# First taps of two depthwise convolutions on ScalarE, and the last step of a SiLU on ScalarE and GpSimd

## The chip, the cores and the metric

The kernel runs on one core of one Trainium2 chip. The metric is the device time of one execution in microseconds (us). The program works on TensorE (PE in the profile, with its weight loads as PEld), VectorE (DVE), ScalarE (ACT) and GpSimd (POOL); SyncE (SP) issues all DMAs. Each engine takes its own instructions in the order in which they were laid down, and semaphores hold an instruction back until its inputs are written and its output buffer is free.

## The reference

Two layers of a hybrid block run over 1024 latent tokens and 256 context tokens of width 1024, all in float32. Each layer normalises and modulates its input, multiplies it by a wide `w_in`, and feeds three branches: a state-space scan (SSD) behind a short convolution, attention with grouped keys, and a conformer branch behind a long convolution. The branches are joined by `w_out`. What matters here is cut to this:

```python
def dwconv(x, w, b):                       # one filter per channel
    y = lax.conv_general_dilated(x, w[:, None, :], (1,), [(pad, pad)], ...)
    return y + b

def ssd_branch(z, xbc, ...):
    xbc = jax.nn.silu(dwconv(xbc, conv_w, conv_b))      # 1280 channels, 5 taps
    ...
def conformer_branch(ua, ub, gate, ...):
    u = ua * jax.nn.sigmoid(ub)
    u = jax.nn.silu(layernorm(dwconv(u, conv_w, conv_b), ln_g, ln_b))   # 512 channels, 31 taps
    u = u @ pw_w + pw_b
    return u * jax.nn.silu(gate)
```

The latent and the context tokens are convolved apart, each padded with zeros. The second layer needs only the latent tokens of the conformer branch.

## The kernel before

A layer has three stages: the input projections (`phase_b`), then attention with the SSD scan woven into it, then the output projection. This change lies in the second half of the first of them. There, channels lie on the 128 partitions and tokens along the free dimension. Every product is a float32 matmul made from three passes over operands split in a high and a low part (`mm3`, lines 210 to 216); the weights of one unit are loaded, rounded to the high part on ScalarE and subtracted to the low part on GpSimd (`wblock`, line 359, tile `wtl`).

The loop over `block(i)` (line 623) takes 17 units of 256 channels each. Units with `xbc` hold two 128-channel slices of the short convolution; there are ten slices, j = 0 to 9. Units with `ub, ua` hold one slice of the conformer branch; there are four. The two kinds alternate, so that two slices of `xbc` are followed by one pair `ub, ua`. After these nine units come eight that only make gates (z, gc, ga).

What happens to a unit is this.

- For `xbc` (line 617), ScalarE copies the matmul results into a padded buffer `xpad` (two buffers, zeroed at the pads by GpSimd). `conv_x` (lines 557 to 588) then makes the first tap with one `tensor_scalar` on VectorE (line 562, product and bias), and four more taps with `scalar_tensor_tensor` (line 565, helper line 208). The SiLU is made from a tanh: ScalarE writes tanh of the result into `th` (line 568), and VectorE makes (th + 1) times the result (line 569); weights and bias carry the factor one half. For j below 8, TensorE then transposes the result (line 582) and ScalarE copies the transposes out for the DMA.
- For `ub` (line 601), ScalarE writes a tanh of the matmul results into a tile that shares the tag `th`, and `th` has one buffer. For `ua` (line 610), VectorE makes (th + 1) times the matmul result into the padded `up`.
- `conv_cm` (lines 549 to 555) then makes 31 taps on VectorE, in place in `cac`: the first with `tensor_scalar` (line 552), thirty with `scalar_tensor_tensor` (line 555, helper line 208). `cac` has 1295 columns in the first layer and 1024 in the second. It is read by TensorE later, in `cm_tail` (line 670).

The matmul results go through four PSUM buffers with tag `m`, so TensorE may run at most four tiles ahead of the engine that empties them.

The order on each engine is not the order of the source. `at(us)` sets a priority, and a planner that simulates the program with its own costs lays down, on each engine, whichever ready instruction has the lowest number. Taps of `conv_cm` are 1.7 apart in these numbers, taps of `conv_x` 2 apart, the tanh of `conv_x` comes at 10 and its transposes at 34 behind the unit's matmuls.

Of the kernel before, what the change touches and what calls it, by code (L numbers as in the profile page):

```python
# [10 lines left out]
AF = mybir.ActivationFunctionType  # L11
ALU = mybir.AluOpType
# [148 lines left out]
def build(tc, a, out, depth=DEPTH, dump=None):  # L161
    nc = tc.nc
    es = ExitStack()
    V, S, G, P, Y = nc.vector, nc.scalar, nc.gpsimd, nc.tensor, nc.sync

    def at(us):
        tc.cur_priority = int(us * 100)
# [6 lines left out]
    def mk(p, shape, tag, dt=F32, bufs=None):  # L174
        uid[0] += 1
        k = {} if bufs is None else {"bufs": bufs}
        return p.tile(shape, dt, tag=tag, name=f"{tag}_{uid[0]}", **k)
# [17 lines left out]
    def tr(o, i, idt):  # L195
        P.transpose(o, i, idt)  # L196

    def act(o, i, f, **k):
        S.activation(o, i, f, **k)  # L199

    def ts(e, o, i, s1, op0, s2=None, op1=None):
        if op1 is None:
            e.tensor_scalar(o, i, s1, None, op0)
        else:
            e.tensor_scalar(o, i, s1, s2, op0, op1)  # L205

    def stt(o, i, s, i1, op0, op1):
        V.scalar_tensor_tensor(o, i, s, i1, op0, op1)  # L208
# [101 lines left out]
    def cc(l, n, j=0, w=1):  # L310
        o = CO[n][0] + j * w
        return colc[l][:, o:o + w]
# [36 lines left out]
    def wblock(p, rp, src, tag, bufs, e=None, rtag="wr", rbufs=1):  # L349
        shape = list(src.shape)  # L350
        hi = mk(p, shape, tag + "h", F32R, bufs=bufs)
        lo = mk(p, shape, tag + "l", F32R, bufs=bufs)
        n = shape[1] // 2
        for k in range(2):
            s = slice(n * k, n * k + n)
            raw = mk(rp, [128, n, shape[2]], rtag, bufs=rbufs)
            Y.dma_start(out=raw, in_=src[:, s])
            act(hi[:, s], raw, AF.Copy)
            (e or G).tensor_tensor(lo[:, s], raw, hi[:, s].bitcast(F32), ALU.subtract)  # L359
        return hi, lo  # L360
# [73 lines left out]
    def phase_b(l, nh, b0, pp):  # L434
# [74 lines left out]
        w = wblock(wt, wt, a["wtm"][l, 1], "wt", 2, V)  # L509
# [3 lines left out]
        for i, j in enumerate((2, 0, 1)):  # L513
            u0 = b0 + 52 + 26 * i
            at(u0 - 20)
            w = wblock(wt, wt, a["wtd"][l] if j == 2 else a["wtm"][l, 2 + j], "wt", 2, V)
# [23 lines left out]
        cw = mk(up_p, [128, 4, 31], "cmw")  # L540
        sw = mk(xp_p, [128, 60], "scw")
# [5 lines left out]
        NCM = 1024 if last else 1295  # L547

        def conv_cm(j, t0, pace):
            u, o = ups[j], cac[j]  # L550
            at(t0)
            ts(V, o[:, 0:NCM], u[:, 0:NCM], cw[:, j, 0:1], ALU.mult, cc(l, "cmb", j), ALU.add)
            for k in range(1, 31):
                at(t0 + k * pace)
                stt(o[:, 0:NCM], u[:, k:k + NCM], cw[:, j, k:k + 1], o[:, 0:NCM], ALU.mult, ALU.add)

        def conv_x(j, t0):
            xp = xps[j]
            at(t0)
            o = mk(xp_p, [128, 1282], "xcv", bufs=2)  # L560
            w = sw[:, 5 * j:5 * j + 5]
            ts(V, o, xp[:, 0:1282], w[:, 0:1], ALU.mult, sw[:, 50 + j:51 + j], ALU.add)
            for k in range(1, 5):
                at(t0 + 2 * k)
                stt(o, xp[:, k:k + 1282], w[:, k:k + 1], o, ALU.mult, ALU.add)
            at(t0 + 10)
            th = mk(up_p, [128, 1282], "th")
            act(th, o, AF.Tanh)
            stt(o, th, 1.0, o, ALU.add, ALU.mult)
            if j >= 6:  # L570
                d = bT_d[j - 6] if j < 8 else cT_d[j - 8]
                Y.dma_start(out=d[:, 0:1024], in_=o[:, 0:1024])
                Y.dma_start(out=d[:, 1024:1280], in_=o[:, 1026:1282])
            if j < 8:
                at(t0 + XLAG)
                sg = mk(gp, [128, NT, 128], "xsg")
                for ta in (0, 4, 8):
                    n = min(4, NT - ta)
                    ps = mk(*((pt, [128, 4, 128], "t") if ta == 4 else (px, [128, 4, 128], "x")))
                    for t in range(ta, ta + n):  # L580
                        c0 = t * 128 + (2 if t >= 8 else 0)
                        tr(ps[:, t - ta, :], o[:, c0:c0 + 128], idf)
                    act(sg[:, ta:ta + n, :], ps[:, 0:n, :], AF.Copy)
                if j < 6:
                    d = xt_d[:, :, 128 * j:128 * j + 128]
                else:
                    d = bt_d[:, :, 128 * (j - 6):128 * (j - 6) + 128]
                Y.dma_start(out=d.rearrange("t p f -> p t f"), in_=sg)
# [34 lines left out]
        def block(i):  # L623
            u = FM_UNITS[i]
            u0 = b2 + 26 * i
            at(u0 - 20)
            w = wblock(wt, wt, a["wfm"][l, i], "wt", 2)
            tt = u0
            for m, (n, j) in enumerate(u):
                full = n == "xbc" or not last  # L630
                for t0, tn in ((0, 512), (512, 512), (1024, 256)):
                    if t0 >= 1024 and not full:
                        continue
                    at(tt)
                    ps = mk(pm, [128, 512], "m")
                    mm3(ps[:, 0:tn], lambda x, k: w[x][:, k, 128 * m:128 * m + 128],
                        lambda x, k: h[x][:, k, t0:t0 + tn], KT)
                    fm_fin(ps, n, j, t0, tn)
                    tt += 5.2 * tn / 512
                if n == "ua":  # L640
                    conv_cm(j, tt, CM_PACE)
                if n == "xbc":
                    conv_x(j, tt)
# [563 lines left out]
```

## Time and profile before

| | |
|---|---|
| time, median of 3 runs | 2924.92 us (2923.34 to 2926.68) |
| the profiled execution's own time | 2925.86 us |
| its span in the trace | 2924.0 us |
| busy over the span: PE, DVE, ACT, POOL | 95%, 74%, 37%, 40% |
| mean granted TensorE clock | 0.976 |

The span runs from the first to the last instruction that was recorded; 1.86 us of the profiled time lie around it. "Busy" is a share of the whole span and hides that the stages have different limits: VectorE is at 9 tenths or more in the convolutions of both layers (about 300 to 605 us and 1814 to 2078 us), and far below that in the gate units behind them. A busy time contains the time in which an instruction has started and is held up inside, so a long duration of a short instruction is itself a sign of something. PEclk is the share of full speed that TensorE was granted.

In timelines a row has the start, the duration, the engine, the line, the operation, the tiles written and read, the shape and the count; a bracket gives the idle time of the engine before it and what ended it. In tables of groups a row has the count, the busy time and the mean duration in ns, then the idle time before. In tables of waits a row has who waited for whom: the total, the number of times and the longest.

### The profile page before, as it was taken

The numbers are of one execution on the slowest core, as the hardware profiler recorded it, in microseconds if no ns is written. First come the engines' busy times: TensorE is split into PE (matmuls) and PEld (weight loads), VectorE is DVE, ScalarE is ACT, GpSimd is POOL, SyncE is SP. The second block draws the span as 40 slices with busy tenths as digits, with TensorE's granted clock in tenths as the row PEclk, the third lists the DMA queues.
The fourth block names the chain that finished last, engine by engine and source line by source line (L and its number), as shares of the span: only waits on it lengthen the run. The fifth ranks groups of instructions, "written<-read, shape, count | busy, mean of one in ns | idle before, by whom it ended". The sixth has DMA issues, their size and how long they took to land. (4 is left out here: it accounts for less than half of the span.)

```text
span 2924.0 us, 41060 instructions
## 1 busy us (share of the span) xinstructions
PE 2775.7 (95%) x15708; PEld 2058.5 (70%) x15708; DVE 2167.2 (74%) x2987; ACT 1068.0 (37%) x1801; POOL 1167.3 (40%) x832
## 2 busy tenths in 40 slices
PE   5999998999999999899999999999998999999998
PEld 3888876888855555565787998877886565555676
DVE  4576899973288889887545577999834889898744
ACT  4212221222245555454335322222223455644532
POOL 2244122232166767662112353122322676775111
PEclk8999998999999999999999999999999999999999
DMA  6541111223342323223745322113335232321654
GB/s 237 191 160 66 56 55 62 92 92 112 101 144 84 102 68 104 67 76 99 213 153 161 122 77 68 56 55 98 111 118 168 74 98 77 95 64 43 185 154 144
DMA packets 284035, 314.44 MB, mean 108 GB/s; under 512 B 27606, under 2 KB 219190, under 8 KB 282814
## 3 DMA queue, kind: packets, MB, share of 16 engines
q1 hardware_dynamic: 283838, 311.82, 33.5%
q8 instruction: 123, 2.02, 0.3%
q14 instruction: 74, 0.61, 0.1%
HBM read 236.25 MB, written 75.50 MB: 107 GB/s over the span
## 5 line engine op out<-in xcount | busy, mean ns | idle before, releaser
L193 PE MATMUL m<-hh,wth 128*128 128x512 f32 (+1 forms) x1440 | 534.9, 371 | 0.1
L193 PE MATMUL m<-hl,wth 128*128 128x512 f32 (+1 forms) x1440 | 533.4, 370 | 0.0
L193 PE MATMUL m<-hh,wtl 128*128 128x512 f32 (+1 forms) x1440 | 532.7, 370 | 0.0
L199 ACT ACTIVATE a_p<-m 128x512 f32<-128x512 f32 x492 | 289.0, 595 | 374.0 <-PE m L193 370.6
L208 DVE SCALAR_TENSOR_TENSOR cac<-up,cmw,cac 128x1295 f32<-128x1295 f32 (+1 forms) x240 | 385.4, 1627 | 2.0
L935 DVE TENSOR_REDUCE a_sm<-m 128x1 f32<-128x512 f32 (+1 forms) x600 | 332.5, 582 | 46.9 <-PE m L193 45.0
L359 POOL TENSOR_TENSOR wtl<-wr,wth 128x1024 fp32r<-128x1024 f32 x68 | 200.3, 2945 | 406.6 <-ACT wth L199 406.6
L193 PE MATMUL t<-a_p,vs 128*64 128x256 f32 x1968 | 324.0, 405 | 0.7 <-DVE a_rc L1010 0.3
L193 PEld LDWEIGHTS m<-hh,wth 128*128 128x128 f32 x1440 | 274.0, 190 | 48.0 <-ACT th L199 0.5
L193 PEld LDWEIGHTS m<-hh,wtl 128*128 128x128 f32 x1440 | 273.5, 190 | 48.3
L193 PEld LDWEIGHTS m<-hl,wth 128*128 128x128 f32 x1440 | 273.8, 190 | 47.4
L193 PE MATMUL m<-q_a,k_a 128*128 128x512 f32 (+1 forms) x656 | 259.7, 406 | 6.1 <-DVE a_sm L935 4.6
L193 PE MATMUL m<-k_a,q_a 128*128 128x512 f32 (+1 forms) x600 | 247.0, 437 | 13.6 <-DVE a_sm L935 9.8
L193 PE MATMUL m<-woh,yh 128*128 128x512 f32 x576 | 225.8, 395 | 8.2 <-issue 3.3
L193 PE MATMUL m<-woh,yl 128*128 128x512 f32 x576 | 228.8, 398 | 4.4 <-DVE yl L1099 4.3
L193 PE MATMUL m<-wol,yh 128*128 128x512 f32 x576 | 226.5, 394 | 0.0
L193 PE MATMUL m<-q_b,k_b 65*128 65x512 f32 (+1 forms) x656 | 218.8, 344 | 0.0
L193 PEld LDWEIGHTS m<-q_a,k_a 128*128 128x128 f32 x656 | 125.9, 192 | 107.1 <-issue 52.0
L193 PEld LDWEIGHTS t<-a_p,vs 128*64 128x64 f32 x1968 | 104.3, 136 | 133.9 <-issue 95.3
L193 PEld LDWEIGHTS m<-k_a,q_a 128*128 128x128 f32 x600 | 113.5, 195 | 113.3 <-issue 45.2
L199 ACT ACTIVATE wth<-wr 128x1024 fp32r<-128x1024 f32 (+1 forms) x84 | 89.3, 1064 | 256.3 <-DMA wr<-in_wfm 134.5
L193 PE MATMUL m<-wth,hh 128*128 128x256 f32 (+1 forms) x608 | 173.7, 288 | 0.6 <-DVE c_qn L474 0.5
(239 smaller groups left out, 5604.4 us busy)
## 6 DMA issues: line engine op xcount, KB each, us to landing
wr<-in_wfm SPq DMA_DIRECT2D x68, 512.0 KB, 3.6
s_cb<-cum_d SPq DMA_DIRECT2D x72, 384.0 KB, 3.7
ada_w<-in_adaw SPq DMA_DIRECT2D x32, 512.0 KB, 4.2
wor<-in_wout SPq DMA_DIRECT2D x64, 256.0 KB, 3.1
s_x<-xt_d SPq DMA_DIRECT2D x38, 384.0 KB, 3.0
yf<-ys_d SPq DMA_DIRECT2D x36, 384.0 KB, 4.0
yf<-ya_d SPq DMA_DIRECT2D x36, 384.0 KB, 4.2
yf<-yc_d SPq DMA_DIRECT2D x36, 256.0 KB, 2.9
```

Source lines behind the costliest of these rows:

```text
L193: P.matmul(o, l, r, start=start, stop=stop)
L199: S.activation(o, i, f, **k)
L208: V.scalar_tensor_tensor(o, i, s, i1, op0, op1)
L359: (e or G).tensor_tensor(lo[:, s], raw, hi[:, s].bitcast(F32), ALU.subtract)
L935: V.tensor_reduce(sm[:, 2 * x + t, j:j + 1], ps[:, 0:kn], axis=AX.X, op=ALU.max)
```

## The change

Four instructions change in the source, in `conv_cm` and `conv_x`.

- The first tap of `conv_cm` (four times a layer) is an activation with function Identity on ScalarE, with the tap as its scale and the bias as its bias, where it was a `tensor_scalar` on VectorE.
- The first tap of `conv_x` (ten times a layer) likewise.
- The last step of the SiLU in `conv_x` (ten times a layer) was one `scalar_tensor_tensor` on VectorE. It is now an Identity with bias 1 on ScalarE, in place in `th`, and a `tensor_tensor` product on GpSimd.

No tile, buffer, priority or DMA is changed. The planner makes its orders anew.

```diff
         def conv_cm(j, t0, pace):
             u, o = ups[j], cac[j]
             at(t0)
-            ts(V, o[:, 0:NCM], u[:, 0:NCM], cw[:, j, 0:1], ALU.mult, cc(l, "cmb", j), ALU.add)
+            act(o[:, 0:NCM], u[:, 0:NCM], AF.Identity, scale=cw[:, j, 0:1], bias=cc(l, "cmb", j))
             for k in range(1, 31):
                 at(t0 + k * pace)
                 stt(o[:, 0:NCM], u[:, k:k + NCM], cw[:, j, k:k + 1], o[:, 0:NCM], ALU.mult, ALU.add)
@@
             w = sw[:, 5 * j:5 * j + 5]
-            ts(V, o, xp[:, 0:1282], w[:, 0:1], ALU.mult, sw[:, 50 + j:51 + j], ALU.add)
+            act(o, xp[:, 0:1282], AF.Identity, scale=w[:, 0:1], bias=sw[:, 50 + j:51 + j])
             for k in range(1, 5):
                 at(t0 + 2 * k)
                 stt(o, xp[:, k:k + 1282], w[:, k:k + 1], o, ALU.mult, ALU.add)
             at(t0 + 10)
             th = mk(up_p, [128, 1282], "th")
             act(th, o, AF.Tanh)
-            stt(o, th, 1.0, o, ALU.add, ALU.mult)
+            act(th, th, AF.Identity, bias=1.0)
+            G.tensor_tensor(o, th, o, ALU.mult)
```

## Prediction

> **What bounds the kernel now.** I read the page first, for the whole, then busy time by stretch, because the change touches one stage of each layer only.
>
> ```profile
> span 2924.0 us, 41060 instructions
> PE 2775.7 (95%) x15708; PEld 2058.5 (70%) x15708; DVE 2167.2 (74%) x2987; ACT 1068.0 (37%) x1801; POOL 1167.3 (40%) x832
> ...
> 300.00:400.00 100.00, 95.85 (x493) 81.08 (x492) 98.29 (x61) 21.80 (x34) 24.15 (x19) 0.98 0.18 58
> 400.00:500.00 100.00, 80.99 (x402) 67.92 (x401) 96.50 (x63) 20.00 (x31) 20.63 (x17) 0.88 0.20 65
> 500.00:605.00 105.00, 102.66 (x530) 86.77 (x529) 103.39 (x72) 19.97 (x30) 24.40 (x7) 1.00 0.23 79
> ...
> 600.00:800.00 200.00, 197.41 (x1051) 168.29 (x1050) 79.82 (x158) 45.92 (x74) 44.99 (x31) 0.99 0.31 106
> ...
> 1900.00:2000.00 100.00, 90.33 (x412) 73.87 (x411) 99.89 (x70) 24.04 (x34) 26.05 (x22) 0.95 0.24 75
> ```
>
> The columns are the stretch, its length, busy time of PE, PEld, DVE, ACT and POOL, the granted clock, and the DMA's share and rate. TensorE sets the time nearly everywhere. In the convolutions (300 to 605, and about 1814 to 2078) VectorE is full and TensorE has holes, while behind them (600 to 800) VectorE falls to 40% and TensorE is full again. The waits of TensorE, 300 to 605 and then 1814 to 2079, say who makes the holes; the row between them is VectorE's only wait from 300 to 605:
>
> ```profile
> PE x L196 <- DVE xcv L208: 13.3, 2, 11.1
> PE x L196 <- ACT xsg L199: 5.7, 3, 4.9
> PE t L196 <- DVE xcv L208: 4.2, 1, 4.2
> PE t L196 <- DVE cac L208: 2.3, 1, 2.3
> ...
> DVE up L208 <- PE m L193: 5.9, 4, 2.7
> ...
> PE t L196 <- DVE xcv L208: 11.7, 3, 6.1
> PE t L196 <- DVE cac L208: 1.2, 1, 1.2
> ```
>
> So 25.5 us in the first layer and 12.9 us in the second are waits for the convolutions, 38.4 us in all. That is the most that a lighter VectorE can give, beside a little clock: 0.88 over 100 us says that some of that stretch ran slowly around its holes.
>
> **What VectorE saves.** Groups, 300 to 605 us, with GpSimd's products for scale, then one row of the second layer:
>
> ```profile
> L205 DVE TENSOR_SCALAR xcv<-xpad,scw 128x1282 f32<-128x1282 f32 x8 | 16.0, 1998 | 0.0
> L208 DVE SCALAR_TENSOR_TENSOR xcv<-th,xcv 128x1282 f32<-128x1282 f32 x8 | 11.9, 1485 | 0.0
> L205 DVE TENSOR_SCALAR cac<-up,cmw,colc 128x1295 f32<-128x1295 f32 x4 | 5.9, 1469 | 0.1
> ...
> L359 POOL TENSOR_TENSOR wtl<-wr,wth 128x1024 fp32r<-128x1024 f32 x19 | 67.9, 3573 | 180.9 <-ACT wth L199 180.8
> ...
> L205 DVE TENSOR_SCALAR cac<-up,cmw,colc 128x1024 f32<-128x1024 f32 x4 | 5.4, 1361 | 0.1
> ```
>
> Read plainly, 16.0 + 11.9 + 5.9 = 33.8 us go. But the means of the first taps are not their price, as the rows below show. (Two of the ten slices come before 300 us, where VectorE has room; they count nothing.)
>
> **What GpSimd's product costs VectorE.** No product of GpSimd stands here on these tiles; the nearest is `wtl`, the same operation on 1024 columns. Timeline:
>
> ```profile
> 338.56 2.55 POOL L359 TENSOR_TENSOR wtl<-wr,wth 128x1024 fp32r<-128x1024 f32 x1 [4.74 <-ACT wth L199]
> 338.78 3.69 DVE L208 SCALAR_TENSOR_TENSOR cac<-up,cmw,cac 128x1295 f32<-128x1295 f32 x1
> ...
> 460.10 8.98 POOL L359 TENSOR_TENSOR wtl<-wr,wth 128x1024 fp32r<-128x1024 f32 x1 [17.65 <-ACT wth L199]
> ...
> 548.43 2.66 POOL L359 TENSOR_TENSOR wtl<-wr,wth 128x1024 fp32r<-128x1024 f32 x1 [4.71 <-ACT wth L199]
> 548.75 0.68 DVE L208 SCALAR_TENSOR_TENSOR g_o<-g_t,m 128x512 f32<-128x512 f32 x1
> 549.35 3.10 DVE L208 SCALAR_TENSOR_TENSOR xcv<-xpad,scw,xcv 128x1282 f32<-128x1282 f32 x1
> ```
>
> The tap that meets `wtl` takes 3.69 us, where the same tap alone takes 1.56 (row 352.63 below): it ends 1.36 us after GpSimd, so it began when GpSimd was done. `g_o`, with one input in PSUM, runs beside GpSimd in 0.68 us; the tap behind it waits. GpSimd and a tap take turns, then, and the other way round GpSimd waits too: 8.98 us where 2.55 do. The slow first taps are such meetings, and when they are gone the next tap meets `wtl` in their place. A first tap's own price is 0.94 us (row 368.33 below; 0.80 for 1024 columns).
>
> The ledger of VectorE, first layer: off go 8 x 0.94 + 4 x 0.94 + 8 x 1.49 = 23.2 us. On come eight products. One costs 3.69 - 1.56 = 2.13 us for 1024 columns, so 2.67 for 1282, and 21.3 us for eight. Net -1.9 us. Second layer: 8 x 0.94 + 4 x 0.80 + 8 x 1.49 = 22.6, net -1.3. The bounds of one product are nothing, where VectorE stands idle anyway, and its whole length, 2.55 x 1282/1024 = 3.2: net between -23.2 and +2.4. I take 2.67, because VectorE has 5.9 us of idleness in 305.
>
> The Trainium skill has this as a rule (SBUF — State Buffer, section "Who interferes with whom"): a VectorE instruction with two SBUF inputs contends with a GpSimd instruction that reads SBUF, and whichever starts first holds the shared ports for its whole length. The trace agrees: 3.69 us with two SBUF inputs, 0.68 with one. By the rule each product that starts first costs the whole 3.2, 4.2 us more per layer than I count.
>
> **What the longer chain costs TensorE.** The hand-over of slices 2 and 3 to TensorE in the first layer, and the same in the second:
>
> ```profile
> 349.91 1.27 ACT L199 ACTIVATE th<-xcv 128x1282 f32<-128x1282 f32 x1 [11.43 <-DVE xcv L208]
> 351.22 1.49 DVE L208 SCALAR_TENSOR_TENSOR xcv<-th,xcv 128x1282 f32<-128x1282 f32 x1
> 352.63 1.56 DVE L208 SCALAR_TENSOR_TENSOR cac<-up,cmw,cac 128x1295 f32<-128x1295 f32 x1
> 352.75 1.36 ACT L199 ACTIVATE th<-m 128x512 f32<-128x512 f32 x3 [1.08 <-DVE xcv L208]
> 352.77 1.12 PE L196 MATMUL t<-msk,xcv 128*128 128x128 f32 x4 [4.15 <-DVE xcv L208]
> 354.11 0.68 DVE L208 SCALAR_TENSOR_TENSOR up<-th,m 128x512 f32<-128x512 f32 x1
> 360.80 0.69 DVE L208 SCALAR_TENSOR_TENSOR up<-th,m 128x512 f32<-128x512 f32 x1 [1.32 <-PE m L193]
> 364.48 0.41 DVE L208 SCALAR_TENSOR_TENSOR up<-th,m 128x256 f32<-128x256 f32 x1
> 364.81 3.59 DVE L208 SCALAR_TENSOR_TENSOR cac<-up,cmw,cac 128x1295 f32<-128x1295 f32 x1
> 368.33 0.94 DVE L205 TENSOR_SCALAR cac<-up,cmw,colc 128x1295 f32<-128x1295 f32 x1
> ...
> 1864.48 1.28 ACT L199 ACTIVATE th<-xcv 128x1282 f32<-128x1282 f32 x1 [11.22 <-DVE xcv L208]
> 1868.36 0.66 PE L196 MATMUL t<-msk,xcv 128*128 128x128 f32 x4 [2.11 <-DVE xcv L208]
> 1868.40 1.09 ACT L199 ACTIVATE th<-m 128x512 f32<-128x512 f32 x2 [2.65 <-DVE xcv L208]
> 1869.41 0.68 DVE L208 SCALAR_TENSOR_TENSOR up<-th,m 128x512 f32<-128x512 f32 x1
> ```
>
> One instruction, the finish at 351.22, frees everything: the transposes on TensorE, and the single `th` buffer into which ScalarE empties three PSUM buffers of `ub`. From tanh to TensorE it takes 2.86 us, in the second layer 3.88. Now come tanh 1.27, Identity, which I price like the tanh on the same shape, 1.27, 0.1 for the extra hand-over (as between tanh and finish here), and the product. For it I take the mean of `wtl` with its waits, 3.573 x 1.252 = 4.47 (bounds 3.2, and 8.98 - 2.55 = 6.4 of waiting more). Together 7.1 us: +4.2 in the first layer, +3.2 in the second. The even slices hand over with room to spare and pay nothing here.
>
> TensorE's delay comes back: the second `up` waits for it already (1.32 us). Per hand-over in the first layer VectorE gains 2 x 0.94 + 1.49 - 2.67 = 0.7 on the way to it, loses 4.2, and gains 0.94 at the first tap of `conv_cm`. That tap waits on ScalarE for the last `up`; the tap of the previous slice (364.81, 3.59 us) covers its 1.27. Without that cover, 1.5 us of idleness take the place of the 0.94. So +2.6 each, and three make +7.7. The last pair, which hands nothing to TensorE, adds 2 x 2.67 - 2 x 0.94 - 2 x 1.49 = +0.5: +8.2. In the second layer the first `up` has 0.46 us of room (1869.41 behind the first half of the pair at 1868.40): -0.7 + 3.2 - 0.46 - 0.80 = +1.2 each, three +3.7, last pair +0.5: +4.2. TensorE waits for the last tap of `cac` at both ends (2.3 and 1.2 us above), so both delays pass on whole.
>
> **What costs nothing.** ScalarE gets 24 more instructions a layer of some 1.27 us, 31 us in a stretch of 305 where it is busy for about 62; nothing on its queue is late but by waiting. The first tap of `conv_x` has its buffers early. Behind that of `conv_cm` stand the next emptyings of `xpad`, with four PSUM buffers in between. Behind the product on GpSimd stand `wtl` (TensorE has no wait for weights above) and pads. The stores of B and C wait on SyncE some 4 us longer with weight loads behind them; that same missing wait is their cover, and without it up to 4 us each would show.
>
> **The sum.** 2925.86 (the profiled execution, 0.94 above the median of the runs and inside their spread) + 8.2 + 4.2 = 2938.3 us. I forecast 2938. With bare products (no wait, 5.8 us for the chain) each of six hand-overs is 1.3 better: 2930. With 2.8 us more of waiting each, half-way between the mean and the worst: 2955.
>
> **The rivals.**
>
> *The room is real (faster).* If the products fall where VectorE stands idle, 23.2 and 22.6 us are truly off. Spread over four pairs that is 5.8 a pair: by the third hand-over 17.4 - 4.2 = 13.2 ahead, and 2.3 at the last tap: -15.5. In the second layer 17.0 - 3.2 = 13.8 exceeds the 11.7 of waits, with 1.2 at the end: -12.9. Together 2897. It decides from the point where a product costs VectorE less than 1.49 + 0.94. For it speaks that VectorE is truly the bound; against it the 3.69 us row. Half of it gives 2911.
>
> *The fillers go (much slower).* Between hand-over and next slice VectorE lives on old taps: seven in the first layer (10.9 us), three of 1.28 in the second (3.8). A planner that takes VectorE to be lighter may lay them ahead of the hand-over. All gone costs 3 x 10.9 + 3 x 3.8 = 44 us, half of it 22, on top of the sum: 2960 to 2982. Against it: no priority is changed.
>
> *It is hidden (no change).* If the new order puts other taps where the chain is longer, the nets remain, -3.2 us: 2923.
>
> **How the numbers follow.** Forecast 0.50 (own range 2930 to 2955), the room is real 0.17, the fillers go 0.13, hidden 0.20. Two runs of this kernel can be told apart from about 0.2%, here 5.8 us. Slower: 0.45 of the first, all 0.13, and 0.02 of hidden, 0.60. Faster: 0.17 and 0.03 of hidden, 0.20. Same: the rest, 0.20. The range 2908 to 2962 leaves out most of the faster case (0.11), the upper half of the fillers (0.06) and 0.02 of the forecast.
>
> **What would show it.** In the profile after, products of GpSimd on `xcv` of about 3.2 us or more, and beside each a tap of some 4.2 us (1.56 + 2.67); about 21 us a layer of such excess. TensorE's transposes of `xcv` waiting for GpSimd, over 25.5 and 11.7 us in total; `up` waiting more than 5.9 us. VectorE's busy share from 300 us to the end of the convolutions unchanged. I am wrong if taps beside the products keep 1.56 us, if TensorE's waits shrink, or if ScalarE's first taps hold up the emptying of PSUM.

## The result, and the profile after

The changed kernel takes 2950.56 us, the median of 4 runs (2946.96 to 2955.21), where the kernel before takes 2924.43 (2923.34 to 2926.68, 4 runs). The ratio is 1.0089, with a 95% interval of 1.0072 to 1.0107: slower by 0.9%. The profiled execution took 2949.53 us, 23.67 more than the profiled execution before. Its page and its busy time by stretch, in the columns of the prediction:

```profile
span 2947.8 us, 41130 instructions
PE 2775.8 (94%) x15708; PEld 2059.3 (70%) x15708; DVE 2131.5 (72%) x2939; ACT 1131.6 (38%) x1849; POOL 1232.2 (42%) x852
...
300.00:400.00 100.00, 92.64 (x477) 78.19 (x477) 99.19 (x57) 31.31 (x41) 26.06 (x21) 0.97 0.16 52
400.00:500.00 100.00, 82.25 (x412) 69.14 (x411) 99.47 (x55) 28.79 (x38) 32.05 (x22) 0.90 0.20 65
500.00:605.00 105.00, 98.13 (x497) 83.31 (x497) 98.31 (x71) 25.70 (x33) 38.45 (x11) 0.97 0.22 75
...
1900.00:2000.00 100.00, 86.05 (x412) 71.25 (x411) 99.36 (x62) 29.43 (x35) 31.13 (x24) 0.95 0.15 52
```

VectorE has 48 instructions less and is as full as it was wherever the convolutions run; over the whole span it is lighter by 36 us. TensorE has the same 2776 us of work and more holes.

Where the time lies is read from one group of matmuls, the first pass of the input projections. Its first and last start in a layer mark the stage. Rows of the tile view, the kernel before, each layer in a window of its own (count, shortest, median and longest in ns, first and last start; the shapes of a large group are those of a sample):

```profile
L193 PE MATMUL m<-hh,wth x816: 274/392/775, 241.6 to 799.0; 128*128 128x512 f32 x109, 128*128 128x256 f32 x55
L193 PE MATMUL m<-hh,wth x624: 274/392/775, 1762.2 to 2226.0; 128*128 128x512 f32 x136, 128*128 128x256 f32 x20
```

The same for the changed kernel:

```profile
L193 PE MATMUL m<-hh,wth x816: 274/392/776, 240.1 to 804.7; 128*128 128x512 f32 x109, 128*128 128x256 f32 x55
L193 PE MATMUL m<-hh,wth x624: 274/392/792, 1768.7 to 2248.7; 128*128 128x512 f32 x136, 128*128 128x256 f32 x20
```

The first layer's stage grew from 557.4 to 564.6 us, +7.2; the second layer's from 463.8 to 480.0, +16.2. Together this is 23.4 of the span's 23.8 us. Below, "the two stages" means the sum of these two lengths: 1021.2 us before, 1044.6 after.

The waits of TensorE in the changed kernel, first 300 to 612 us, then 1814 to 2092:

```profile
PE x L196 <- ACT xsg L199: 19.1, 3, 7.5
PE t L196 <- DVE cac L208: 6.9, 1, 6.9
PE x L196 <- POOL xcv L570: 6.0, 3, 2.0
...
PE t L196 <- POOL xcv L570: 17.7, 3, 7.3
PE t L196 <- DVE cac L208: 9.0, 1, 9.0
```

The rows for `xsg` belong to the hand-overs: ScalarE's copies of an even slice's transposes stand in its order behind the tanh and Identity of the odd slice (in the first one below, at 351.77 behind 350.60), and TensorE needs the PSUM buffer that they empty. With them the hand-overs of `xcv` hold TensorE for 25.1 us in the first layer (23.2 before) and 17.7 us in the second (11.7 before). The wait for the last tap of `cac` went from 2.3 to 6.9 us and from 1.2 to 9.0. So there are two sources, and the larger is the second: +7.9 us at the hand-overs, +12.4 us at the end of the long convolution. Together 20.3 of 23.4. The other 3 us are no idleness: in the two stages TensorE is busy 985.7 us for the same matmuls, 982.6 before. That fits the first matmuls behind a wait, which take longer than later ones of the same kind (0.78 us at 356.71 and 0.39 at 358.12, both shown below).

Now the pieces. GpSimd's product on an even slice, and the tap beside it (timeline of the changed kernel), then the groups, 300 to 605 us:

```profile
331.55 3.85 POOL L570 TENSOR_TENSOR xcv<-th,xcv 128x1282 f32<-128x1282 f32 x1 [0.34 <-ACT th L199]
332.61 4.16 DVE L208 SCALAR_TENSOR_TENSOR cac<-up,cmw,cac 128x1295 f32<-128x1295 f32 x1
...
L208 DVE SCALAR_TENSOR_TENSOR cac<-up,cmw,cac 128x1295 f32<-128x1295 f32 x120 | 230.4, 1932 | 3.8 <-ACT cac L199 1.9
L208 DVE SCALAR_TENSOR_TENSOR xcv<-xpad,scw,xcv 128x1282 f32<-128x1282 f32 x32 | 59.7, 1866 | 0.0
L570 POOL TENSOR_TENSOR xcv<-th,xcv 128x1282 f32<-128x1282 f32 x8 | 28.7, 3591 | 12.2 <-ACT th L199 12.2
```

The tap ends 1.37 us after the product, so it ran when GpSimd was done, as the tap beside `wtl` did before. Eight taps of the first layer carry such an excess, 20.7 us over their own price, and eight of the second, 20.5. The same 120 and 32 taps took 209.6 and 53.1 us before: they are 27.4 us dearer now, a part of it meetings with `wtl` that fell on the first taps before. VectorE's busy time from 300 to 605 us is 297.0 us, against 298.2; the second window holds some gate work too, since the convolutions now end earlier.

The hand-over of slices 2 and 3 in the first layer, and one of the second:

```profile
349.12 8.87 DVE L208 SCALAR_TENSOR_TENSOR cac<-up,cmw,cac 128x1295 f32<-128x1295 f32 x4
349.29 1.27 ACT L199 ACTIVATE th<-xcv 128x1282 f32<-128x1282 f32 x1 [13.37 <-DVE xcv L208]
350.60 1.27 ACT L199 ACTIVATE th<-th 128x1282 f32<-128x1282 f32 x1
352.01 3.02 POOL L570 TENSOR_TENSOR xcv<-th,xcv 128x1282 f32<-128x1282 f32 x1 [2.52 <-ACT th L199]
355.06 1.36 ACT L199 ACTIVATE th<-m 128x512 f32<-128x512 f32 x3 [1.55 <-POOL xcv L570]
355.09 1.12 PE L196 MATMUL x<-msk,xcv 128*128 128x128 f32 x4 [1.99 <-POOL xcv L570]
356.71 0.78 PE L193 MATMUL m<-hh,wth 128*128 128x512 f32 x1
357.91 0.68 DVE L208 SCALAR_TENSOR_TENSOR up<-th,m 128x512 f32<-128x512 f32 x1
...
1869.92 1.28 ACT L199 ACTIVATE th<-xcv 128x1282 f32<-128x1282 f32 x1 [11.59 <-DVE xcv L208]
1872.65 3.75 POOL L570 TENSOR_TENSOR xcv<-th,xcv 128x1282 f32<-128x1282 f32 x1 [2.54 <-ACT th L199]
1876.43 0.60 ACT L199 ACTIVATE th<-m 128x512 f32<-128x512 f32 x1 [3.92 <-POOL xcv L570]
```

From tanh to the first emptying behind it: 5.77 us (355.06 - 349.29), 2.84 before; 6.51 in the second layer, 3.92 before. But VectorE does not wait behind it. At 349.12 it has four old taps in front of the `up`, and reaches that `up` at 357.91, 2.85 us after its input was begun.

The `cac` wait has another origin. Between the third hand-over and the transposes that wait for `cac`, TensorE has projections. Their count before, first and second layer (windows 494.0 to 604.8 and 1985.7 to 2078.0):

```profile
L193 PE MATMUL m<-hh,wth x178: 274/392/775, 496.0 to 602.3; 128*128 128x512 f32 x120, 128*128 128x256 f32 x58
L193 PE MATMUL m<-hh,wth x132: 274/392/775, 1986.4 to 2075.9; 128*128 128x512 f32 x116, 128*128 128x256 f32 x16
```

And after (windows 494.5 to 595.2 and 1999.7 to 2081.4), with the spacing of such matmuls:

```profile
L193 PE MATMUL m<-hh,wth x153: 274/392/775, 496.5 to 587.9; 128*128 128x512 f32 x104, 128*128 128x256 f32 x49
L193 PE MATMUL m<-hh,wth x108: 274/392/774, 2000.4 to 2072.1; 128*128 128x512 f32 x92, 128*128 128x256 f32 x16
...
358.12 0.39 PE L193 MATMUL m<-hh,wth 128*128 128x512 f32 x1
358.81 0.40 PE L193 MATMUL m<-hh,wth 128*128 128x512 f32 x1
```

In the new order the transposes stand 16 matmuls of 512 columns and 9 of 256 earlier in the first layer, 24 of 512 earlier in the second. Each stands for three passes, 0.69 us at 512 columns: some 14 us (16 x 0.69 + 9 x 0.35) and 17 us (24 x 0.69) of work that used to lie ahead of them. VectorE's last tap came earlier too, but by less. Before, then after, first layer:

```profile
L208 DVE SCALAR_TENSOR_TENSOR cac<-up,cmw,cac x120: 1550/1559/3707, 300.6 to 603.3; 128x1295 f32<-128x1295 f32 x120
```

```profile
L208 DVE SCALAR_TENSOR_TENSOR cac<-up,cmw,cac x120: 1550/1565/4169, 299.9 to 593.7; 128x1295 f32<-128x1295 f32 x120
```

It is 9.6 us earlier, the transposes 14: the difference is the 4.6 us by which that wait grew. In the second layer the last tap ends 3.5 us later (2078.0 before, 2081.5 after), although the whole stage began 6.5 later, so VectorE is 3.0 us ahead there. The hand-overs hold TensorE back by 6.0 more. 17 - 3.0 - 6.0 leaves about the 7.8 by which that wait grew.

### The profile page after: what moved, and what is told of

It reads as the page before. It is cut to its first block, busy times and chain, and to the rows that moved or that the text cites. A ratio compares the mean times of both kernels' runs of the same rounds, so it can differ in the third digit from the quotient of the medians.

```text
span 2947.8 us, 41130 instructions
## 1 busy us (share of the span) xinstructions
PE 2775.8 (94%) x15708; PEld 2059.3 (70%) x15708; DVE 2131.5 (72%) x2939; ACT 1131.6 (38%) x1849; POOL 1232.2 (42%) x852
## 5 line engine op out<-in xcount | busy, mean ns | idle before, releaser
L208 DVE SCALAR_TENSOR_TENSOR cac<-up,cmw,cac 128x1295 f32<-128x1295 f32 (+1 forms) x240 | 433.0, 1817 | 7.6 <-ACT cac L199 3.7
L359 POOL TENSOR_TENSOR wtl<-wr,wth 128x1024 fp32r<-128x1024 f32 x68 | 193.7, 2849 | 259.1 <-ACT wth L199 248.1
```

## The experiments

Each was timed in several rounds against the kernel before on the same chip. In the first four runs the kernel before took 2928.19 us (median of 22 runs, 2918.36 to 2934.26), in the last four 2927.14 (median of 32, 2917.03 to 2937.46). These runs scatter more than those of the result, and only the ratios are compared. Diffs are against the changed kernel.

### The first taps alone, the SiLU as before

```diff
-            act(th, th, AF.Identity, bias=1.0)
-            G.tensor_tensor(o, th, o, ALU.mult)
+            stt(o, th, 1.0, o, ALU.add, ALU.mult)
```

> The first taps of both convolutions on ScalarE, the SiLU's last step left on VectorE as before. Theory (GpSimd and VectorE's taps take turns; the longer chain from tanh to TensorE; transposes of cac that TensorE's order has earlier): neither the product nor the longer chain is here. VectorE loses 8 x 0.94 + 4 x 0.94 = 11.3 us in the first layer and 10.7 in the second, and nothing comes on. The waits of TensorE shrink by most of that: 2905 to 2912 us, faster than before by 13 to 20. Taps of 4.2 us are gone, those of 3.6 us beside wtl stay. Rival (the 14 first taps on ScalarE hold up the emptying of PSUM or make VectorE wait): some half of the 26 us that the whole change lost, 2935 to 2940.

Measured: 2918.15 us, ratio 0.9970 (0.9954 to 0.9985). The two stages take 1010.1 us, 11.1 less than before, but in this one execution the attention between them took 8.9 us longer (972.1 against 963.2); see the table of steps below. The hand-overs of the first layer hold TensorE for 14.5 us instead of 23.2, but the wait for `cac` rose to 3.8 us there and to 6.7 us in the second layer. In the second layer TensorE also waits 4.3 us for ScalarE to empty a PSUM buffer into `th`. So this half of the change is worth 0.3%, somewhat less than expected.

### The SiLU alone, the first taps as before

```diff
-            act(o[:, 0:NCM], u[:, 0:NCM], AF.Identity, scale=cw[:, j, 0:1], bias=cc(l, "cmb", j))
+            ts(V, o[:, 0:NCM], u[:, 0:NCM], cw[:, j, 0:1], ALU.mult, cc(l, "cmb", j), ALU.add)
...
-            act(o, xp[:, 0:1282], AF.Identity, scale=w[:, 0:1], bias=sw[:, 50 + j:51 + j])
+            ts(V, o, xp[:, 0:1282], w[:, 0:1], ALU.mult, sw[:, 50 + j:51 + j], ALU.add)
```

> The SiLU's last step on ScalarE and GpSimd, the first taps left on VectorE. Theory: each of ten products a layer costs a tap beside it 2.6 us and saves 1.49, so VectorE is heavier than before by 8 x 1.1 = 9 us a layer in the full stretch, and the chain to TensorE is longer by 4 us at each of six hand-overs: slower than the whole change or like it, 2950 to 2965 us. Rival (ScalarE's first taps are what cost): 2930 to 2938, between before and the whole change.

Measured: 2964.72 us, ratio 1.0117 (1.0099 to 1.0134), inside the expectation; the two stages take 1052.9 us, 31.7 more than before. The loss is in the SiLU alone, and the taps give back a part of it.

### The product on VectorE

```diff
-            G.tensor_tensor(o, th, o, ALU.mult)
+            V.tensor_tensor(o, th, o, ALU.mult)
```

> The whole change, but the SiLU's product is made by VectorE; th + 1 stays on ScalarE. Theory: no product of GpSimd, so no turn-taking; VectorE loses only its first taps, 11 us a layer; the chain to TensorE is longer than before by one ScalarE instruction, 1.3 us, at six hand-overs: 2908 to 2920 us, faster than before. Taps of 4.2 us are gone. Rival (ScalarE's 24 instructions a layer cost, wherever the product is): 2945 to 2955, like the whole change.

Measured: 2930.55 us, ratio 1.0004 (0.9994 to 1.0015). The turns with GpSimd's product are gone (those with `wtl` stay), and so is most of the loss, but the gain of the first taps did not come out either: the expectation was missed by 10 us. The third hand-over of the first layer in this run shows one reason:

```profile
482.02 5.26 DVE L208 SCALAR_TENSOR_TENSOR cac<-up,cmw,cac 128x1295 f32<-128x1295 f32 x2
482.19 1.27 ACT L199 ACTIVATE th<-xcv 128x1282 f32<-128x1282 f32 x1 [1.69 <-DVE xcv L208]
483.49 1.27 ACT L199 ACTIVATE th<-th 128x1282 f32<-128x1282 f32 x1
487.20 1.49 DVE L570 TENSOR_TENSOR xcv<-th,xcv 128x1282 f32<-128x1282 f32 x1
488.72 1.36 ACT L199 ACTIVATE th<-m 128x512 f32<-128x512 f32 x3 [2.56 <-DVE xcv L570]
```

The chain is 6.53 us long here. Two taps fill the two activations, they meet `wtl`, and the product stands behind them until 487.20. Where nothing is met the chain is 4.43 us, still 1.6 longer than before: one activation of 1.27 us more, and its hand-overs.

### The tail of the long convolution 20 priority units later

`cm_tail` holds the transposes of `cac`.

```diff
-TAIL = 40.0
+TAIL = 60.0
```

> The whole change, with the conformer's tail laid 20 later in priority (TAIL 60 for 40), which puts the transposes of cac into TensorE's order about where they were before the change. Theory: the two waits of TensorE for the last tap of cac (6.9 and 9.0 us, 2.3 and 1.2 before) go, because TensorE has 2.4 and 2.6 tiles of 5.6 us more to do ahead of them: 12 to 16 us faster than the whole change, 2935 to 2940. What is left of the loss is the hand-overs of xcv. Rival (the delay is VectorE's and only shows there): TensorE waits elsewhere instead, no change, 2948 to 2953.

Measured: 2937.07 us, ratio 1.0030 (1.0017 to 1.0043). The waits of TensorE in this run, first and second layer:

```profile
PE x L196 <- ACT xsg L199: 18.7, 3, 6.7
PE x L196 <- POOL xcv L570: 6.0, 3, 2.0
PE m L193 <- DVE g_o L208: 1.2, 1, 1.2
...
PE t L196 <- POOL xcv L570: 16.7, 3, 6.9
```

The hand-overs are as long as in the changed kernel, and the waits for `cac` are gone. The two stages take 1027.9 us, 16.7 less than those of the changed kernel; the ratio is 0.59% lower. That is the share of the early transposes in the changed kernel.

It is the share in this kernel only, because the planner moved them furthest here. The number of `m<-hh,wth` matmuls from the start of the stage to the transposes that need the last tap is, for the first and second layer:

| run | matmuls ahead |
|---|---|
| kernel before | 546, 452 |
| first taps alone | 544, 440 |
| product on VectorE | 542, 441 |
| SiLU alone | 537, 436 |
| changed kernel | 521, 428 |
| changed kernel, late tail | 544, 448 |

With both parts of the change, which take the most off VectorE, the transposes come earliest.

### The same late tail with the first taps alone, and with the kernel before

> First taps on ScalarE, SiLU as before, and the conformer's tail 20 later in priority. Theory: the taps-only kernel gained 10 us instead of 13 to 20 because TensorE's order had the transposes of cac 1.5 tiles earlier in the second layer and waited 3.8 and 6.7 us for the last taps. Laid one tile later there, the 6.7 goes almost wholly, the 3.8 stays in part: 6 to 8 us faster than taps-only, 2910 to 2914 beside a kernel before of 2928, ratio about 0.994 to 0.996; faster than both kernels. Rival (VectorE's end sets it, wherever the wait shows): as taps-only, ratio 0.997.

> The kernel before with the conformer's tail 20 later in priority and nothing else. Theory: TensorE waits for cac only 2.3 and 1.2 us there, so at most 3.5 us can be had: ratio 0.998 to 1.000. Rival (a late tail is worth some 13 us on any kernel, and has nothing to do with the change): ratio about 0.996.

Measured: 2916.88 us, ratio 0.9970 (0.9958 to 0.9981), and 2927.87 us, ratio 1.0005 (0.9994 to 1.0017). The late tail does nothing for the kernel before, so the 0.59% are no general gain of a later tail. For the first taps alone the expectation was missed: the `cac` wait of the second layer is gone in the profile, and the two stages are 4.0 us shorter than without the late tail (1006.1 against 1010.1), but the ratio is the same. 4 us are 0.14%, and these intervals cannot tell them. The late tail had little to move there, 1 and 8 matmuls against 23 and 20 in the changed kernel. The ratio is that of the rival, which this run does not refute.

### Half a product

GpSimd multiplies columns 0 to 640 only; the late tail stays.

```diff
-            G.tensor_tensor(o, th, o, ALU.mult)
+            G.tensor_tensor(o[:, 0:641], th[:, 0:641], o[:, 0:641], ALU.mult)
```

> The whole change with the late tail, and GpSimd multiplies only the first 641 of the 1282 columns (the other columns stay without the SiLU's factor). TensorE's order has the transposes of cac at the same places as in the whole change with the late tail. Theory: the cost goes with the length of the product. Taps beside it take 2.9 us where 4.2 were (1.55 + half of 2.6); the excess is 10 us a layer where it was 20.6; the chain from tanh to TensorE is 1.5 us shorter, 4.3 and 5.0 us. Together 8 to 15 us faster than the whole change with the late tail (ratio 1.003): ratio 0.998 to 1.000. Rival (an instruction more on GpSimd and ScalarE and their hand-overs cost, whatever the length): ratio 1.003, unchanged.

Measured: 2923.89 us, ratio 0.9990 (0.9981 to 0.9998). One product of it:

```profile
353.40 1.66 POOL L570 TENSOR_TENSOR xcv<-th,xcv 128x641 f32<-128x641 f32 x1 [2.53 <-ACT th L199]
```

The cost goes with the length of the product: 0.40% lie between this run and the full product with the same tail (1.0030). No count of instructions or of hand-overs differs between the two. A tap that meets only such a half product takes 1.2 us more than its own price, where one beside a full product took 2.6 more.

### The product on VectorE, with the late tail

> The whole change with the late tail and the product on VectorE, nothing of it on GpSimd. Again the transposes of cac lie at the same places. Theory: no excess of taps beside products; chain 4.4 and 5.2 us as in the run with the product on VectorE; the waits for cac (4.1 and 7.5 us there) go: ratio 0.995 to 0.998, faster than that run (1.0004) by 8 to 11 us, and slower than taps-only with the late tail by some 4 to 8 us, for one ScalarE instruction at six hand-overs. Rival (ScalarE's extra instructions are what costs): ratio 1.003.

Measured: 2928.19 us, ratio 1.0002 (0.9991 to 1.0013). The late tail gave nothing here, and the expectation was missed. It had only 2 and 7 matmuls to move, and the waits for `cac` fell from 4.1 and 7.5 us to 2.5 and 2.5 without a gain in time. With the transposes late, one more activation in the chain still takes back all that the first taps give.

Three of these runs have the transposes of `cac` at the same place in TensorE's order, within one matmul, and differ in the SiLU only. Their stages, from the tile view. The first taps alone:

```profile
L193 PE MATMUL m<-hh,wth x816: 274/392/776, 243.7 to 790.5; 128*128 128x512 f32 x109, 128*128 128x256 f32 x55
L193 PE MATMUL m<-hh,wth x624: 274/392/796, 1757.5 to 2216.8; 128*128 128x512 f32 x136, 128*128 128x256 f32 x20
```

With Identity and the product on VectorE:

```profile
L193 PE MATMUL m<-hh,wth x816: 274/392/775, 241.7 to 794.0; 128*128 128x512 f32 x109, 128*128 128x256 f32 x55
L193 PE MATMUL m<-hh,wth x624: 274/392/775, 1767.3 to 2231.2; 128*128 128x512 f32 x136, 128*128 128x256 f32 x20
```

With Identity and the product on GpSimd:

```profile
L193 PE MATMUL m<-hh,wth x816: 274/392/775, 241.6 to 799.2; 128*128 128x512 f32 x109, 128*128 128x256 f32 x55
L193 PE MATMUL m<-hh,wth x624: 274/392/776, 1768.4 to 2238.7; 128*128 128x512 f32 x136, 128*128 128x256 f32 x20
```

So the way from the kernel before to the changed one can be walked in four steps. The first column is one profile each, the second the ratios of the runs.

| step | two stages | ratio |
|---|---|---|
| first taps on ScalarE, late tail | 1021.2 to 1006.1: -15.1 | -0.30% |
| Identity ahead of the product (on VectorE) | to 1016.2: +10.1 | +0.32% |
| the product from VectorE to GpSimd | to 1027.9: +11.7 | +0.28% |
| the tail back at 40, transposes early | to 1044.6: +16.7 | +0.59% |
| sum | +23.4 | +0.89% |

The second column times 2927 us is -8.8, +9.4, +8.2 and +17.3. Both agree but for the first step, where the two stages show more than the runs. By the whole spans of these profiles (2924.0, 2916.2, 2926.7, 2935.0 and 2947.8 us) the steps are -7.8, +10.5, +8.3 and +12.8: the first now agrees, because the attention between the two stages took 967.0 us there and 963.2 before. It took 973.3, 969.2 and 964.0 in the next three. Whether that follows from the edits or is scatter of single executions is open, so the last step is worth between 12.8 us (spans) and 17.3 (ratios).

The table is one order of the steps, and the steps depend on each other. With the tail at 40 the product's move from VectorE to GpSimd costs 0.85% (1.0004 to 1.0089), and it also brings the transposes 21 and 13 matmuls further ahead. Of the 10.1 us of the second step, 5.6 are idleness of TensorE and 4.6 the same matmuls taking longer, so the waits of the longer chain show for about half of it.

## Why the prediction was right, and where it was not

The direction and its first cause held: the forecast was 2938 against 2950.56 measured, the gain taken off VectorE was eaten by the product, and the hand-overs became longer. Its size was half of the measured one, for one step that failed. That the time still fell so close in the first layer is luck: the sum led the cost through a delay of VectorE that did not occur.

*GpSimd's product beside a tap: held.* 2.67 us each was forecast, 21.3 us for eight; 20.7 and 20.5 were measured. The ledger held too: from the first tap of `conv_cm` with two inputs to the end of the last, taps and SiLU together take 2.7 us less of VectorE's time in the first layer and 0.9 less in the second, where -1.9 and -1.3 were forecast. The Trainium skill says the same of such a move (Perfetto Trace Analysis, section "Optimizing Scalar/DVE Operations"): offloading between GpSimd and VectorE might not help, because they share a read port. The runs agree: with the late tail, the product is 0.28% cheaper on VectorE than on GpSimd.

*The chain: right in kind, too long.* 7.1 us was forecast, 5.77 and 6.51 were measured. The mis-sized term is the product with its waits, 4.47 us by the mean of `wtl`; inside the hand-overs it took 3.01 to 3.76. `wtl` as a mean contains long waits that no product inside a hand-over met. (The upper bound's 2.8 us of waiting, half-way between the mean of 4.47 and the worst of 3.2 + 6.4 = 9.6, is 2.6 by these numbers, and its 2955 is 2954; nothing hangs on it.)

*TensorE's delay comes back into VectorE: wrong.* `up` was to wait more than 5.9 us. VectorE's waits of 300 to 605 us have no row for `up` any more; the one row for `cac` is this:

```profile
DVE cac L208 <- ACT cac L199: 1.9, 1, 1.9
```

The planner laid more old taps ahead of the hand-over (the 8.87 us at 349.12), so that VectorE had other work while the chain ran. In the first layer VectorE ended 9.6 us earlier, not later. In the second, `up` waits 7.2 and 4.9 us at 1813.78 and 1819.37, which is ahead of the taps of `conv_cm`, and not behind a hand-over. The row above is the price that the prediction named for a first tap of `conv_cm` without cover, 1.5 us; it is paid once a layer, not at each slice.

*"TensorE waits for the last tap of cac at both ends, so both delays pass on whole": this is the step that failed.* It held TensorE's order fixed. The planner moved the transposes of `cac` some 14 and 17 us of work ahead, and the waits for the last tap grew by 4.6 and 7.8 us. With the tail later in the priorities this part goes, 16.7 us of 23.4 by the profile and 0.59% of 0.89% by the runs. That the planner did so because its costs see VectorE lighter, and do not contain the turns with GpSimd, fits the table of matmuls ahead, where the transposes come earlier with each piece of work that leaves VectorE; no run shows the planner's costs, so the reason is argued, not shown.

*The layers.* +8.2 and +4.2 were forecast, +7.2 and +16.2 came. The first agrees by accident: 1.9 us at the hand-overs and 4.6 at the tail stand in place of three delays and a last pair. In the second layer the hand-overs pay 6.0 us and the tail 7.8, where the sum had 4.2 for both. Its last tap came later, when that of the first layer came 9.6 earlier, because its stage began 6.5 us later; VectorE itself needed 1.6 us less from the first tap of `conv_cm` with two inputs to the end of the last (261.2 to 259.6 us). In the first layer it needed 8.8 less (304.2 to 295.4), and 5.9 of that are the waits for `up`, which are gone.

*ScalarE's instructions cost nothing: half right.* Alone, the first taps made the kernel faster by 0.3%. But Identity is not free: it lies in the one chain that TensorE waits for, and with the product on VectorE adding it costs 0.32%, about half of it seen as idleness of TensorE.

*The rivals.* "The room is real" needs products that cost less than the work removed, and the 4.16 us tap refutes it; the first taps alone have such room, and their 0.3% are 9 us, of 2897's 29. "Hidden" falls with the hand-overs' waits, longer in both layers. "The fillers go" came nearest to the mechanism: a planner that takes VectorE to be lighter lays things ahead. What it laid ahead were TensorE's transposes; of the taps that it did move ahead of the hand-over the waits show no harm.

A version that beats both kernels is the first taps alone, 0.9970 of the kernel before (0.9954 to 0.9985). A second buffer for `th`, which would take the emptying of PSUM out of the chain, was not tried.

## What to carry to other kernels

Work that leaves VectorE for GpSimd is paid by VectorE all the same where its own instructions read two tiles in SBUF; measure one such pair in the old trace before you count a gain. Before you lengthen a chain that another engine waits for, ask what else is freed by its end, here transposes and four PSUM buffers. And where a planner makes the order, a change on one engine moves the instructions of all others: compare the two orders first, since an unchanged priority does not keep an instruction in its place.

## What was not expected of the hardware

GpSimd is held up much longer by taps in a row than by one. From the timeline of the changed kernel:

```profile
535.32 11.70 POOL L359 TENSOR_TENSOR wtl<-wr,wth 128x1024 fp32r<-128x1024 f32 x1 [16.98 <-ACT wth L199]
...
543.22 1.55 DVE L208 SCALAR_TENSOR_TENSOR xcv<-xpad,scw,xcv 128x1282 f32<-128x1282 f32 x1
544.69 0.68 DVE L208 SCALAR_TENSOR_TENSOR g_o<-g_t,m 128x512 f32<-128x512 f32 x1
545.28 3.10 DVE L208 SCALAR_TENSOR_TENSOR cac<-up,cmw,cac 128x1295 f32<-128x1295 f32 x1
```

`wtl` takes 11.70 us, where the same instruction took 2.55 at its best in the prediction's rows. All taps from 535.85 to 544.77 kept their own price of 1.55 or 1.56 us, so they went ahead of it one after another. It ended at 547.02, 2.33 us behind the start of `g_o`, which has one input in PSUM. That is about its own length, so GpSimd seems to have got its turn when VectorE did not need two inputs from SBUF. The Trainium skill (SBUF — State Buffer, section "Who interferes with whom") says that the one that issues first holds the shared ports for its whole instruction and the other blocks. The rows agree for one pair. In a row of taps, who comes next is not the one that has waited longest: `wtl` stood there from 535.32, and the six taps that went ahead of it all began later.

The traces give a hint. In a row of taps each starts some 0.08 us before the end of the one ahead (544.69 against 543.22 + 1.55). At some places there is a pause instead. There the next tap starts some 0.04 us behind the end. Counted over all pairs of taps in the ten traces where a product or `wtl` had begun before the first tap ended and before the second began, and ended after the first: after a pause GpSimd had the next turn (the second tap was held up) 164 times of 164, without one 117 times of 252. Whether the pause lets GpSimd in or only shows that it came in, no run here tells.
